# A hybrid decoder layer on one core: attention stages entered at a pair's first product, gate loads as a step, one x block made earlier, output operands on other x blocks

## Chip, cores and metric

One core of a Trainium2 chip runs the kernel. The metric is device time in microseconds (us); a time of the kernel is the median of its runs. TensorE (PE) has two granted clock levels in these records, 2.4 GHz (1.0) and 1.2 GHz (0.5). PE multiplies, VectorE (DVE) and ScalarE (ACT) prepare weights and take results away, SyncE (SP) issues nearly all DMAs. Each engine executes its own queue in the order in which the program puts the instructions there, and waits at the first one whose operands are not ready.

## What is computed

```python
xn = rmsnorm(h, g_pre)                       # h: 16 meta tokens + 512 tokens, 2048 wide
p = xn @ w_in                                # columns: q k v z_gla r hc gate_b gate_c z_conv
q, k, v, z_gla, r, hc, gate_b, gate_c, z_conv = split(p)
log_a = log_sigmoid(r @ w_gate_up + b_gate) / 16
o = gla_chunked(q * 128 ** -0.5, k, v, log_a)   # 4 heads, S_t = diag(exp(log_a)) S + k^T v
y_gla = rmsnorm(o, g_gla_out) * silu(z_gla)
y_conv = gate_b * causal_dwconv(gate_c * hc, w_conv) * silu(z_conv)
y = concat([y_gla, y_conv]) @ w_out
out = (h + rmsnorm(y, g_post))[16:]
```

All is float32. The kernel keeps that precision by splitting each operand into a rounded high half and the rest (low half) and summing three products: high by high, high by low, low by high.

## The kernel before

**Pairs and products.** The columns of `w_in` are cut into tiles of 128. After a start that multiplies six tiles plainly, two tiles at a time form a `Pair` (names such as `k1q1`, `z4z5`), and the pair is computed by a scheme of seven half-size products instead of eight, in the order `P5 P1 P6 P2 P3 P7 P4` (line 38). Each product needs one block of x, made once as high and low halves (`block`, line 502; arrays `xa`, `xb`, `xt`), and one block of weights per pair. A product is 24 matmuls of 256 to 264 columns: eight slices times three half-products. P2 accumulates onto the PSUM bank of P1 and P3 onto that of P5, so P2 can start only when ACT has copied P1's result away (`q`, line 256), and P3 only when it has copied P5's (`f`, line 253).

**Preparing weights.** `prepare` (line 202) adds or subtracts two raw tiles on DVE where the scheme wants it (P5, P6 and P3 at line 183, P7 at line 213), then `split` (line 114) makes the high half on ACT (`whi`, line 118) and the low half on DVE (`wlo`, line 119), into three buffers each. Next-pair loads are issued in the `prepare` of P5, P6 and P4 alone. The main loop (line 729) prepares two products ahead (`AHEAD = 2`), multiplies, and calls `away` (line 248), which takes results away.

**Attention stages.** Five generators per head are woven into the pairs: `decay` (letter d, line 583; nine steps, mostly DVE and three table functions on ACT), `gla_b` (t, transposes and scores), `gla_c` (s, states), `gla_d` (o, output and its norm) and `gla_e` (g, gate: loads `silu(z)` from DRAM, transposes, multiplies). A step ends at a `yield`. `away` runs `per` steps after each product and all that is left after P4. `before` stages enter at P5 and must be through at P2; `stages` enter at P2 (line 262). Which head's stages ride on which pair is the table at lines 358 to 367. Finished gates `silu(z)` go to DRAM (`zd`, line 301) and come back in `gla_e` (line 716); the two `z` buffers serve both.

**Order.** The program hands its instructions to a scheduler that puts them in order on each engine, with later code able to pass earlier code where it fits; the listings in the section on the change show the result.

**End.** After the last pair (`b7s7`) the mixed operand `ycat` is split into `ygh, ygl, ych, ycl` (lines 741 to 747), in the memory that the x blocks leave free, and PE computes the output projection in 16 blocks of 48 matmuls, 512 columns wide.

Of the kernel before, what the change touches and what calls it, by code (L numbers as in the profile page):

```python
# [9 lines left out]
F32 = mybir.dt.float32  # L10
# [5 lines left out]
P = 128  # L16
D = 2048
# [10 lines left out]
NP = S // P  # L28
# [3 lines left out]
XHALF = L // 2  # L32
NB = 8
# [9 lines left out]
def hymba_kernel(ctx, tc, xT, x, g_pre, w_r, w_t, w_up, b_gate, g_gla, w_conv, w_o, g_post, out):  # L43
# [10 lines left out]
    g1 = left.enter_context(tc.tile_pool(name="g1", bufs=1))  # L54

    def bank(name):
        return ps.tile([P, 512], F32, tag="bank", name=name)

    def mm(out_, lhsT, rhs, start, stop, **kw):
        nc.tensor.matmul(out_, lhsT, rhs, start=start, stop=stop, **kw)  # L60
# [36 lines left out]
    xa = [xp.tile([P, 2, NB, XHALF], F32R, tag=f"xa{i}", name=f"xa{i}") for i in range(2)]  # L97
# [70 lines left out]
    left_over = []  # L168
    STAGE = {}
# [3 lines left out]
    def step(n):  # L173
        for _ in range(n):
            while left_over:
                try:
                    next(left_over[0])
                    break
                except StopIteration:
                    left_over.pop(0)  # L180
# [4 lines left out]
    class Pair:  # L185
# [37 lines left out]
        def multiply(self, name, two):  # L223
            hi, lo = two
            (xh, xl), s = xc[name]
            c0, w = self.c0, self.w
            bank_of = {"P2": "P1", "P3": "P5"}.get(name)
            if bank_of:
                pt = self.sb[bank_of]
            else:  # L230
                pt = bank(f"{self.na}{self.nb}{name}")[:, 0:w]
                self.sb[name] = pt
            kw = {"skip_group_check": True} if bank_of else {}
            for k in range(NB):
                mm(pt, hi[:, k, :], xh[:, s, k, c0:], k == 0 and not bank_of, False, **kw)
                mm(pt, hi[:, k, :], xl[:, s, k, c0:], False, False, **kw)
                mm(pt, lo[:, k, :], xh[:, s, k, c0:], False, k == NB - 1, **kw)
# [10 lines left out]
        def away(self, name):  # L248
            sb = self.sb
            if name == "P5":  # L250

                left_over.extend(STAGE[g[0]](int(g[1])) for g in self.before)
                A.copy(self.tmp("f"), sb["P5"])
            elif name == "P1":

                A.copy(self.tmp("q"), sb["P1"])
            elif name == "P6":
                V.tensor_tensor(out=self.tmp("u"), in0=sb["P6"], in1=sb["q"], op=ALU.subtract)
            elif name == "P2":
                if self.before:  # L260
                    step(1000)
                left_over.extend(STAGE[g[0]](int(g[1])) for g in self.stages)
                self.dst_a, self.dst_b = self.dst()
                for o, s, e in self.dst_a[0]:
                    A.copy(o, sb["P1"][:, s - self.c0:e - self.c0])
            elif name == "P3":
                self.put(self.dst_a[1], sb["P5"], sb["u"], ALU.subtract)
            elif name == "P7":
                v = self.tmp("v")
                V.tensor_tensor(out=v, in0=sb["u"], in1=sb["P7"], op=ALU.subtract)  # L270
                self.put(self.dst_b[1], v, sb["f"], ALU.subtract)
            else:
                self.put(self.dst_b[0], sb["v"], sb["P4"], ALU.subtract)

    def prepare_next():
        n = len(ready)
        if n < len(line):
            p, i, name = line[n]
            at = line.index((p, 0, ORDER[0])) + len(ORDER)
            ready.append(p.prepare(name, line[at][0] if at < len(line) else None))  # L280
# [16 lines left out]
    def silu(*js):  # L297
        for j in js:
            z = zs.pop(j)
            A.activation(z, z, AF.Silu)  # L300
            nc.sync.dma_start(zd[:, j, :], z)
# [4 lines left out]
    def k_q(h, **kw):  # L306
        Pair(f"k{h}", f"q{h}", 0, lambda: (new_k(h), new_q(h)), **kw)

    def v_v(h, **kw):
        Pair(f"v{2 * h}", f"v{2 * h + 1}", 0, lambda: (new_v(2 * h), new_v(2 * h + 1)), **kw)  # L310

    def z_z(h, **kw):
        Pair(f"z{2 * h}", f"z{2 * h + 1}", NM // 2, lambda: (new_z(2 * h), new_z(2 * h + 1)),
             done=lambda: silu(2 * h, 2 * h + 1), **kw)
# [42 lines left out]
    def all_pairs():  # L357
        z_z(1)
        k_q(1, before=("d0",), per=3)
        v_v(1, before=("t0",), stages=("s0", "o0"))  # L360
        z_z(2, stages=("g0", "d1"), per=3)
        k_q(2, stages=("t1", "s1", "o1"), per=3)
        v_v(2, stages=("g1", "d2"), per=3)
        z_z(3, stages=("t2", "s2", "o2"), per=3)
        k_q(3, stages=("g2",))
        v_v(3, stages=("d3",))
        conv(0, ("t3", "s3"), ("o3", "g3"))
        for j in range(1, 8):
            conv(j)


    with tc.tile_pool(name="ini", bufs=1, reuse_waits="tile") as ini:
# [43 lines left out]
        for kt in range(KT):  # L416
# [7 lines left out]
            if kt == 10:  # L424
                for n in range(2):
                    t = slice(n * XHALF, (n + 1) * XHALF)
# [16 lines left out]
        def new_k(h):  # L443
            kn[h] = g1.tile([P, L], F32, tag="kn", name="kn")
            return natural(kn[h])

        def new_q(h):
            qn[h] = g1.tile([P, L], F32, tag="qn", name="qn")[:, 0:S]
            return main_only(qn[h])

        def new_v(j):
            t = g1.tile([P, L], F32, tag=f"vt{j % 2}", name="vt")
            vt.setdefault(j // 2, []).append(t)
            return natural(t)

        def new_z(j):
            zs[j] = gla.tile([P, S], F32, tag="z", name="z", bufs=2)
            return main_only(zs[j])
# [43 lines left out]
        def block(name, two, s, src):  # L502
            xc[name] = (two, s)
            for k in HK:
                A.copy(two[0][:, s, k, :], src[:, k])
                V.tensor_tensor(out=two[1][:, s, k, :], in0=src[:, k],
                                in1=two[0][:, s, k, :].bitcast(F32), op=ALU.subtract)
# [13 lines left out]
        tt = ini.tile([P, NB, XHALF], F32, name="tt")  # L521
# [12 lines left out]
        do_plain("z1", None)  # L534
        silu(0, 1)
        all_pairs()
        prepare_next()
        prepare_next()
        block("P1", xa, 0, b11)
        multiply(0)  # L540
        prepare_next()
        block("P2", xb, 0, b21)
# [1 line left out]
        prepare_next()  # L544
        multiply(2)
        block("P3", xb, 1, b22)
        prepare_next()
        block("P4", xa, 1, tt)
        first = 3


# [160 lines left out]
    def gla_e(h):  # L712
        on = st[h]
        zt = [gla.tile([P, S], F32, tag="z", name="z", bufs=2) for _ in range(2)]
        for e in range(2):
            nc.sync.dma_start(zt[e], zd[:, 2 * h + e, :])
        for e in range(2):
            ot = bank(f"ot{h}{e}")
            for p in range(NP):
                nc.tensor.transpose(ot[:, p * P:(p + 1) * P], on[:, p, e * P:(e + 1) * P], ident)  # L720
            z = zt[e]
            V.scalar_tensor_tensor(out=z, in0=ot, scalar=gg[:, e:e + 1], in1=z,
                                   op0=ALU.mult, op1=ALU.mult)
            nc.sync.dma_start(yd[:, 2 * h + e, :], z)
            yield


    STAGE.update(d=decay, t=gla_b, s=gla_c, o=gla_d, g=gla_e)
    for n in range(len(line)):
        while len(ready) < min(len(line), n + 1 + AHEAD):  # L730
            prepare_next()
        if n >= first:
            multiply(n)
        away(n)
# [3 lines left out]
    NC = 4  # L738
    NW = D // NC
    yp2 = ctx.enter_context(tc.tile_pool(name="yp2", bufs=1, side="right", reuse_waits="tile"))  # L740
    ygh, ygl, ych, ycl = (yp2.tile([P, 8, S], F32R, name=n) for n in ("ygh", "ygl", "ych", "ycl"))
    yg = yp2.tile([P, NP, D], F32, name="yg")
    for hi, lo, src in ((ygh, ygl, ycat["g"]), (ych, ycl, ycat["c"])):
        for k in range(0, 8, 2):
            A.copy(hi[:, k:k + 2], src[:, k:k + 2])  # L745
# [119 lines left out]
```

## Time and profile before

| | |
|---|---|
| median of 3 runs | 842.11 us (841.1 to 842.98) |
| profiled execution | 844.2 us, of it 842.5 us span |
| mean granted PE clock | 0.988 |
| busy: PE, DVE, ACT | 812.3, 621.1, 394.7 us |

The span is the time from the first to the last instruction. A view of waits says for how long an engine stood still and which instruction of which engine ended that. In a timeline each line is start, duration, engine, line of the code, operation, operands; what stands in brackets is idle time just before it and its releaser. A fast DVE operation may be recorded as longer than the distance to the next one's start; the distance is what it costs in a full queue.

### The profile page before, as it was taken

The page shows a single profiled execution, that of the slowest core. Times are in us where ns is not written, and L with a number is a line of the kernel's source. Part 1 is how long each engine was busy: PE and PEld are TensorE (multiplying, and loading weights), DVE is VectorE, ACT ScalarE, POOL GpSimd, SP SyncE. Part 2 cuts the span into 40 slices and gives each one's busy share as a digit, 9 for nine tenths or more (in the row PEclk, how much of TensorE's full clock was granted, in tenths as well). Part 3 has the DMA queues.
Part 4 walks back from the last instruction along what each step waited for, and adds up shares of the span by engine and source line. Part 5 has one row for each costly group of instructions (what it writes and reads, how often), then busy time and mean ns, then how long its engine had stood idle before and what let it go on. Part 6 is the DMA issues. An engine that isn't in the chain of part 4 may idle for free.

```text
span 842.5 us, 14191 instructions
## 1 busy us (share of the span) xinstructions
PE 812.3 (96%) x5980; PEld 769.4 (91%) x5980; DVE 621.1 (74%) x770; ACT 394.7 (47%) x547; POOL 2.3 (0%) x14
## 2 busy tenths in 40 slices
PE   8999898998989998999999999999998999999996
PEld 7999898997989998999999999999998788888886
DVE  6999989788799778979888878787877723140433
ACT  7635575485475465454444444444445622130311
POOL 0000000000000000000000000000000000000000
PEclk9999999998999999999999999999999999999999
DMA  8612222243133431263333333333334705050154
GB/s 288 210 52 86 96 96 98 76 151 114 62 117 127 156 104 50 76 224 102 101 101 119 105 115 115 118 106 100 102 100 145 274 19 187 1 200 0 51 182 168
DMA packets 30560, 98.92 MB, mean 117 GB/s; under 512 B 3904, under 2 KB 4800, under 8 KB 29728
## 3 DMA queue, kind: packets, MB, share of 16 engines
q1 hardware_dynamic: 28912, 94.86, 34.2%
q10 hardware_dynamic: 1584, 3.15, 1.0%
q8 instruction: 47, 0.77, 0.4%
q14 instruction: 17, 0.14, 0.1%
HBM read 89.61 MB, written 8.39 MB: 116 GB/s over the span
## 4 chain that ended last, share of the span: by engine, by line
PE 82%; DVE 8%; ACT 5%; issue 3%; DMA 2%; SPq 0%; DVEq 0%; ACTq 0%
PE out L60 21%; PE v L60 3%; PE k3q3P L60 2%; PE v2v3P L60 2%; PE h7c7P L60 2%; PE h5c5P L60 2%; PE h2c2P L60 2%; PE h6c6P L60 2%; PE h4c4P L60 2%; PE h3c3P L60 2%; PE h1c1P L60 2%; PE b3s3P L60 2%; PE b6s6P L60 2%; PE b5s5P L60 2%; PE b4s4P L60 2%
## 5 line engine op out<-in xcount | busy, mean ns | idle before, releaser
L118 ACT CAST whi<-raw 128x1024 fp32r<-128x1024 f32 x207 | 216.4, 1051 | 222.7 <-DVE raw L183 94.2
L119 DVE TENSOR_TENSOR wlo<-raw,whi 128x1024 fp32r<-128x1024 f32 x207 | 251.9, 1222 | 49.1 <-ACT whi L118 45.3
L183 DVE TENSOR_TENSOR raw<-raw 128x1024 f32<-128x1024 f32 x75 | 90.1, 1221 | 4.6 <-DMA raw<-in_w_t_dram 3.8
L791 DVE TENSOR_TENSOR yg<-out,gpost 128x512 f32<-128x512 f32 (+1 forms) x17 | 11.2, 659 | 110.3 <-ACT junk L790 110.2
L790 ACT ACTIVATE junk<-out 128x512 f32<-128x512 f32 (+1 forms) x17 | 9.7, 572 | 120.7 <-PE out L60 120.7
L60 PE MATMUL out<-whi,ygh 128*128 128x512 f32 (+1 forms) x136 | 52.0, 386 | 2.5 <-ACT ygh L745 2.5
L60 PE MATMUL out<-whi,ygl 128*128 128x512 f32 (+1 forms) x136 | 52.7, 388 | 0.3 <-DVE ygl L746 0.3
L60 PE MATMUL out<-wlo,ygh 128*128 128x512 f32 (+1 forms) x136 | 52.5, 386 | 0.0
L60 PE MATMUL out<-wlo,ych 128*128 128x512 f32 (+1 forms) x136 | 51.9, 381 | 0.0
L60 PE MATMUL out<-whi,ych 128*128 128x512 f32 (+1 forms) x136 | 51.9, 381 | 0.0
L60 PE MATMUL out<-whi,ycl 128*128 128x512 f32 (+1 forms) x136 | 51.9, 381 | 0.0
L60 PEld LDWEIGHTS out<-whi,ygh 128*128 128x128 f32 x136 | 25.9, 191 | 8.3 <-ACT ygh L745 2.7
L60 PEld LDWEIGHTS out<-whi,ygl 128*128 128x128 f32 x136 | 25.9, 190 | 6.4 <-DVE ygl L746 0.8
L60 PEld LDWEIGHTS out<-wlo,ygh 128*128 128x128 f32 x136 | 25.9, 191 | 5.6
L213 DVE TENSOR_TENSOR raw<-raw 128x1024 f32<-128x1024 f32 x25 | 30.6, 1223 | 0.6
L60 PEld LDWEIGHTS out<-wlo,ych 128*128 128x128 f32 x136 | 25.5, 188 | 5.5
L60 PEld LDWEIGHTS out<-whi,ycl 128*128 128x128 f32 x136 | 25.5, 188 | 5.5
L60 PEld LDWEIGHTS out<-whi,ych 128*128 128x128 f32 x136 | 25.5, 187 | 5.5
L129 ACT CAST whi<-raw 128x1024 fp32r<-128x1024 f32 (+2 forms) x13 | 11.0, 850 | 20.2 <-PE v L60 12.5
L60 PE MATMUL k2q2P<-xt,whi 128*128 128x264 f32 x48 | 10.3, 315 | 4.0 <-ACT whi L118 4.0
L130 DVE TENSOR_TENSOR wlo<-raw,whi 128x1024 fp32r<-128x1024 f32 (+2 forms) x13 | 12.5, 970 | 0.8 <-ACT whi L129 0.8
L60 PE MATMUL h0c0P<-xt,whi 128*128 128x258 f32 x48 | 10.4, 316 | 2.8 <-ACT whi L118 2.8
(663 smaller groups left out, 2319.4 us busy)
## 6 DMA issues: line engine op xcount, KB each, us to landing
raw<-in_w_t_dram SPq DMA_DIRECT2D x108, 512.0 KB, 4.1
raw<-in_w_o_dram SPq DMA_DIRECT2D x32, 512.0 KB, 4.8
xres<-in_x_dram SPq DMA_DIRECT2D x4, 1024.0 KB, 6.4
xr<-in_xT_dram SPq DMA_DIRECT2D x7, 528.0 KB, 6.5
z<-zd SPq DMA_DIRECT2D x8, 256.0 KB, 3.7
yd<-z SPq DMA_DIRECT2D x8, 256.0 KB, 3.7
yg<-yd SPq DMA_DIRECT2D x1, 2048.0 KB, 8.1
out_dram<-yg SPq DMA_DIRECT2D x8, 256.0 KB, 2.5
```

Source lines behind the costliest of these rows:

```text
L60: nc.tensor.matmul(out_, lhsT, rhs, start=start, stop=stop, **kw)
L118: A.copy(hi, raw)
L119: V.tensor_tensor(out=lo, in0=raw, in1=hi.bitcast(F32), op=ALU.subtract)
L129: A.copy(hi[:, k, :], raw[:, k, :])
L130: V.tensor_tensor(out=lo[:, k, :], in0=raw[:, k, :], in1=hi[:, k, :].bitcast(F32), op=ALU.subtract)
L183: V.tensor_tensor(out=a, in0=a, in1=b, op=ALU.add)
L213: V.tensor_tensor(out=raw["11"], in0=raw["11"], in1=raw["22"], op=ALU.subtract)
L790: nc.scalar.activation(junk, pt, AF.Square, accum_out=s_)
L791: nc.vector.tensor_tensor(out=yg[:, t, cs], in0=pt, in1=gpost[:, cs], op=ALU.mult)
```

## The change

Four edits. (1) A pair's `stages` now enter at P5 if the pair has no `before` stages, and the pairs that had `per=3` without `before` fall back to two steps per product. (2) `gla_e` yields once after issuing its two loads, so that loads and transposes are different steps. (3) In the start of the paired part, `block("P4", ...)` moves from the end to a place right after `block("P1", ...)`, and one `prepare_next()` (that of the first pair's P3) is dropped there, so that the main loop prepares it. (4) In the memory of the x blocks, `yg` now comes first, over the two `xa` arrays, and `ygh, ygl, ych, ycl` after it, on `xb` and `xt`.

```diff
             if name == "P5":
-                left_over.extend(STAGE[g[0]](int(g[1])) for g in self.before)
+                left_over.extend(STAGE[g[0]](int(g[1])) for g in self.before or self.stages)
                 A.copy(self.tmp("f"), sb["P5"])
...
                 if self.before:
                     step(1000)
-                left_over.extend(STAGE[g[0]](int(g[1])) for g in self.stages)
+                    left_over.extend(STAGE[g[0]](int(g[1])) for g in self.stages)
...
-        z_z(2, stages=("g0", "d1"), per=3)
-        k_q(2, stages=("t1", "s1", "o1"), per=3)
-        v_v(2, stages=("g1", "d2"), per=3)
-        z_z(3, stages=("t2", "s2", "o2"), per=3)
+        z_z(2, stages=("g0", "d1"))
+        k_q(2, stages=("t1", "s1", "o1"))
+        v_v(2, stages=("g1", "d2"))
+        z_z(3, stages=("t2", "s2", "o2"))
...
         block("P1", xa, 0, b11)
+        block("P4", xa, 1, tt)
         multiply(0)
...
         block("P3", xb, 1, b22)
-        prepare_next()
-        block("P4", xa, 1, tt)
         first = 3
...
             nc.sync.dma_start(zt[e], zd[:, 2 * h + e, :])
+        yield
...
+    yg = yp2.tile([P, 4 * NB * XHALF], F32, name="yg")[:, 0:NP * D].rearrange(
+        "p (t d) -> p t d", d=D)
     ygh, ygl, ych, ycl = (yp2.tile([P, 8, S], F32R, name=n) for n in ("ygh", "ygl", "ych", "ycl"))
-    yg = yp2.tile([P, NP, D], F32, name="yg")
```

How the order on the engines moves, at the three places that the prediction speaks of. First ACT at the first pair, `z2z3`; `whi<-raw` is the high half of a weight block, `f` and `q` are the copies that P3 and P2 wait for:

```order
 L300 ACTIVATE raw<-raw 128x512
-L118 CAST whi<-raw 128x1024 x3
-L253 COPY f<-z2z3P_1028 128x256
-L256 COPY q<-z2z3P_1064 128x256
-L118 CAST whi<-raw 128x1024
-L265 COPY z<-z2z3P_1064 128x256
+L118 CAST whi<-raw 128x1024 x2
+L253 COPY f<-z2z3P_1032 128x256
+L256 COPY q<-z2z3P_1068 128x256
+L118 CAST whi<-raw 128x1024 x2
+L265 COPY z<-z2z3P_1068 128x256
```

The two copies now stand before the third high half (P3's), no longer behind it.

DVE at the same place before, from the last x blocks of P3 (`xb`) on; `xa<-tt` is half of P4's block, `u` takes P6 away, L213 is P7's subtraction:

```order
L506 TENSOR_TENSOR xb_100<-xr,xb_99 128x1056 x2
L183 TENSOR_TENSOR raw<-raw 128x1024
L506 TENSOR_TENSOR xa_98<-tt,xa_97 128x1056
L119 TENSOR_TENSOR wlo<-raw,whi 128x1024
L258 TENSOR_TENSOR u<-z2z3P_1093,q 128x256
```

Here P4's half block stands ahead of P3's low half (the L119). The same stretch after, from the same x blocks to P3's low half:

```order
L506 TENSOR_TENSOR xb_100<-xr,xb_99 128x1056 x2
L183 TENSOR_TENSOR raw<-raw 128x1024
L258 TENSOR_TENSOR u<-z2z3P_1097,q 128x256
L213 TENSOR_TENSOR raw<-raw 128x1024
L119 TENSOR_TENSOR wlo<-raw,whi 128x1024
```

P4's half block has left this stretch (it stands earlier), and P3's low half now comes behind `u` and P7's subtraction.

DVE around the pair `z4z5`, which carries gate g0 and decay d1, before; the rows run from the result of P7 (`v`) into the next pair's weights:

```order
L270 TENSOR_TENSOR v<-u,z4z5P_2087 128x256
L604 TENSOR_TENSOR eqk<-B 128x512
L607 TENSOR_TENSOR esx<-B 128x512
L610 TENSOR_TENSOR esx<-B 128x16
L612 TENSOR_TENSOR esx<-B 128x4x64
L613 TENSOR_TENSOR esx<-B 128x4x64
L119 TENSOR_TENSOR wlo<-raw,whi 128x1024
L722 SCALAR_TENSOR_TENSOR z<-ot_2019,gg,z 128x512
L246 TENSOR_TENSOR z<-v,f 128x256
```

The decay's exponents (L604 on) and the gate's second half (L722) stand behind P7's result here. After, in the middle of the same pair, from P6's result (`u`) to P7's low half:

```order
L258 TENSOR_TENSOR u<-z4z5P_1978,q 128x256
L596 TENSOR_TENSOR esx<-B,esx 128x528
L213 TENSOR_TENSOR raw<-raw 128x1024
L119 TENSOR_TENSOR wlo<-raw,whi 128x1024
L597 SCALAR_TENSOR_TENSOR B<-keep,esx 128x528
L119 TENSOR_TENSOR wlo<-raw,whi 128x1024
```

The decay's operation on the logarithm (now L596) has moved ahead of P7's subtraction (L213) and P3's low half (the first L119), its scan (L597) between that and P7's low half, and its exponents follow there; both gate operations stand further up.

## Rows read from the trace of the kernel before

**Rows 1.** Waits of PE: waiting line, releaser: total us, times, longest.

```profile
PE k2q2P L60 <- ACT whi L118: 4.0, 1, 4.0
PE h0c0P L60 <- ACT whi L118: 2.8, 1, 2.8
PE z2z3P L60 <- ACT f L253: 2.6, 1, 2.6
PE out L60 <- ACT ygh L745: 2.5, 1, 2.5
...
PE z6z7P L60 <- ACT whi L118: 1.6, 1, 1.6
PE z6z7P L60 <- DVE wlo L119: 1.5, 1, 1.5
```

**Rows 2.** Four stretches: length, busy (x count) by engine, PEclk, DMA share, GB/s.

```profile
96.00:103.00 7.00, 4.41 (x26) 4.20 (x25) 6.92 (x8) 2.64 (x4) 0.53 (x1) 0.76 0.23 82
...
191.00:202.00 11.00, 7.00 (x40) 6.57 (x39) 9.44 (x13) 6.70 (x10) 0.00 (x0) 0.69 0.42 134
245.00:254.00 9.00, 5.93 (x48) 5.41 (x48) 8.49 (x13) 5.61 (x11) 0.00 (x0) 1.00 0.16 60
319.00:332.00 13.00, 9.58 (x65) 9.06 (x65) 11.81 (x17) 6.51 (x12) 0.00 (x0) 0.87 0.14 40
```

**Rows 3.** Timeline of ACT at the first pair.

```profile
97.50 1.04 ACT L118 CAST whi<-raw 128x1024 fp32r<-128x1024 f32 x1 [5.02 <-DVE raw L183]
...
98.72 0.38 ACT L256 COPY q<-z2z3P 128x256 f32<-128x256 f32 x1
```

**Rows 4.** Timeline of DVE at the first pair.

```profile
97.31 1.25 DVE L506 TENSOR_TENSOR xa<-tt,xa 128x1056 fp32r<-128x1056 f32 x1
98.58 1.23 DVE L119 TENSOR_TENSOR wlo<-raw,whi 128x1024 fp32r<-128x1024 f32 x1
99.72 0.42 DVE L258 TENSOR_TENSOR u<-z2z3P,q 128x256 f32<-128x256 f32 x1
100.06 1.22 DVE L213 TENSOR_TENSOR raw<-raw 128x1024 f32<-128x1024 f32 x1
```

**Rows 5.** Pieces of the chain that ended last: start us, us, what.

```profile
411.21 20.03 PE h2c2P L60 x168
```

**Rows 6.** The same chain at 286 us, the transposes of one gate.

```profile
286.13 0.87 PE ot L720 x8
```

**Rows 7.** Timeline of ACT in `z4z5`: the decay's first functions.

```profile
177.64 0.86 ACT L591 ACTIVATE esx<-zp,bg 128x264 f32<-128x264 f32 x2
178.52 1.28 ACT L595 ACT_TABLE_LOAD   x1
179.81 0.65 ACT L595 ACTIVATE esx<-esx 128x528 f32<-128x528 f32 x1
```

**Rows 8.** Timeline of DVE at the end of decay d1.

```profile
192.92 0.69 DVE L633 TENSOR_TENSOR B<-B,qn 128x512 f32<-128x512 f32 x1
193.52 1.22 DVE L183 TENSOR_TENSOR raw<-raw 128x1024 f32<-128x1024 f32 x1
...
195.85 2.36 DVE L119 TENSOR_TENSOR wlo<-raw,whi 128x1024 fp32r<-128x1024 f32 x2 [0.51 <-ACT whi L118]
```

**Rows 9.** The chain that ended last at 185 us: a gate's load.

```profile
185.75 3.25 DMA z<-zd
```

**Rows 10.** DMA issues by line: engine, operation, count, KB each, us to landing.

```profile
z<-zd SPq DMA_DIRECT2D x8, 256.0 KB, 3.7
...
zd<-z SPq DMA_DIRECT2D x6, 256.0 KB, 2.8
```

**Rows 11.** The tile `z`, all its DMAs.

```profile
DMA to landing us min/median/max: 2.0/3.1/5.6
```

**Rows 12.** Timeline of ACT after the last pair.

```profile
651.64 0.62 ACT L344 ACTIVATE sg<-sg 128x512 f32<-128x512 f32 x1
652.17 1.98 ACT L745 CAST ygh<-yg 128x1024 fp32r<-128x1024 f32 x2
```

## Prediction

> **What bounds the kernel now.** I read the table of busy times first: PE works 812.3 of 842.5 us, so a change can only win what PE loses. The view of PE's waits [rows 1] tells where: nearly all of its long waits end with a weight half made by ACT or DVE, and they lie where a pair that carries a decay ends and the next begins (`k2q2`, `z6z7`, `h0c0`), at the first pair (`z2z3`) and before the output projection (`out`). The windows around four of these places [rows 2] give what each costs. Idle time is length less PE's busy time: 2.6 us at the first pair, 4.0 at `k2q2`, 3.1 at `z6z7`, 3.4 at `h0c0`. DVE is busy for most of each window (6.92 of 7.00 at the first pair). The PEclk column shows a second loss: a mean of 0.76 over 7 us is 7 x 0.24 / 0.5 = 3.4 us at the lower level (1.2 GHz), 0.69 over 11 us is 6.8 us, 0.87 over 13 us is 3.4 us; at `z6z7` it stays 1.00. Work at the lower level takes twice its time, so of the part in which PE works half is lost: 1.5 of about 3 us after the restart at the first pair, 2.5 of about 5 at `k2q2` (restart near 196, when the whi of [rows 8] is there), 1.7 at `h0c0`. Together the places cost 4.1 (A, first pair), 6.5 (C, `k2q2`), 3.1 (D, `z6z7`) and 5.1 us (E, `h0c0`).
>
> For scale: an undisturbed pair of seven products takes 20.03 us [rows 5], so a product 2.86 and a matmul 0.12.
>
> **Edit 3, the first pair (A).** Before, P6's end is followed by 2.6 us of waiting for ACT's copy `f` [rows 1], since ACT, in its queue, sat idle for 5.0 us in front of P3's high half at 97.50 and made the copies only behind it, at 98.45 and 98.72 [rows 3]. Now the copies stand ahead of that cast, both sources are long done, and P2 starts when P6 ends, at 96.3. The wait does not vanish: P3 is next. P3's low half ran from 98.58 [rows 4]; in the new order P4's half block (97.31 to 98.58) has moved ahead, at equal cost in a queue that is full anyway, while `u` and P7's subtraction (99.72 to 101.2 together, 0.34 + 1.14) come ahead of it. So it ends at about 99.8 + 1.5 = 101.3. PE has P2 until 99.15 and three matmuls (0.36) that need high halves alone: it waits 101.3 - 99.15 - 0.36 = 1.8 us, in pieces, as the third of these also needs P7's high half. Gain 4.1 - 1.8 = **2.3 us**, if the clock holds through pieces of that size. The dropped `prepare_next` issues no load (only P5, P6 and P4 do), so no queue is passed by a DMA.
>
> **Edits 1 and 2 at `z4z5`, which sets C.** Removed: nothing; the nine decay steps and the gate cost DVE and ACT the same, and no table load goes or comes. What moves is the start, from P2 to P5, four products or so less crowding at the end. Before, the next pair's P6 addition stood behind the whole decay, from 193.52 on, and its low half came after 195.85 [rows 8]. Before, DVE also waited for a gate's operand, whose load began at 185.75 and took 3.25 us [rows 9] because it was asked for only then; with edit 2 and the earlier start the loads stand in SP's queue right behind the stores that free their buffers, two pairs ahead, so g0 finds its operand there.
>
> Two points must now be met. *First, P3's low half.* PE passes the gate's first transposes after P5, the second and the decay's two small matmuls after P1. From there ACT needs 0.9 for the absolute values, 1.3 for a table load, 0.55 for the exponential [rows 7], and as much again for the logarithm: 4.6 us. Then DVE, where L596 is ahead in the queue: 0.6 for a 512-wide operation (spacing from 192.92 to 193.52 in [rows 8]), 1.14 for P7's subtraction, 1.14 for P3's low half (spacing 98.58 to 99.72 [rows 4]): 7.5 us. Behind that L596 are queued P7's and P3's weights, and PE waits for those. PE has P6, P2 and three matmuls meanwhile, 5.7 + 0.4 = 6.1: it waits **1.4 us**. *Second, the next pair's P6.* From P3's low half on DVE has five low halves and one addition (6 x 1.14), the rest of the decay (a scan of some 1.2, seven 512-wide at 0.6, four 256-wide at 0.34 and a tiny one: 6.9), four evictions at 0.34 and one transposed operand of 0.5: 15.6 us. PE has the rest of P3 (2.6), P7, P4 and two products of the next pair (11.4) and fourteen transposes (1.5, at 0.87 for eight [rows 6]): 15.5 us. Level: I allow **0.5 us** for waits between the engines. C then costs 1.9 instead of 6.5: gain **4.6 us**.
>
> **`v4v5` (D) and `v6v7` (E).** `v4v5` carries g1 and d2 in the same order, `v6v7` d3 without a gate and with the decay a product earlier. By likeness both keep 1.9 us: gains 3.1 - 1.9 = **1.2** and 5.1 - 1.9 = **3.2 us**. The bounds of that 1.9: 0 where DVE gets ahead, 4.6 if the whole function chain is exposed. `k1q1` and `v2v3` (1.8 and less on waits) keep their rows and their cost.
>
> **Gate g2 in `k3q3`, a new wait.** It now starts at P5, directly behind the pair that makes z6 and z7. z7 is finished at about 2.6 us after that pair's P4 (eviction, table load 1.28, function 0.65), then its store takes 2.8 and the load 3.7 [rows 10]: 9.1. DVE waits for it at the second gate operation, and behind that stand P7's subtraction and P3's low half: with 0.7 + 2 x 1.14 that is 12.1 to 12.6. PE needs that half after four products, one gate's transposes and two matmuls: 11.4 + 0.9 + 0.2 = 12.5. I take **0.5 us** lost; if both transfers land as late as the slowest, 5.6 [rows 11], it is 4 us more. SP's raw loads behind these transfers need buffers that come free later still; without that cover each would wait 2.8.
>
> **Edit 4, the output operands: zero.** ACT begins the first split at 652.17, directly behind the gate's silu at 651.64 [rows 12]. What holds it is its place in ACT's queue, not the memory, and its place is the same in the new order. The 2.5 us of `out` [rows 1] stay.
>
> **Sum.** 2.3 + 4.6 + 1.2 + 3.2 - 0.5 = 10.8 us off the span of 842.5, about 831.7; the 1.7 us between span and profiled execution do not change. The median of runs, 842.1, is close to the span: **831.3 us**. The forecast's own range is 828 to 835.
>
> **A rule against it.** The load of a table takes 1.28 us and the function follows 0.01 us later, at 179.81 [rows 7]. The Trainium skill (ScalarE: Activation LUTs, section What ACT_TABLE_LOAD costs) counts some 1.38 us of drain on top, about 2.66 us a switch. By it the function chain would be 2.8 us longer, and as an estimate from that page the three pairs would lose 8 us more. This trace shows no such drain behind the load, so the sum goes by the rows.
>
> **Rivals.**
> *The clock falls in the new waits.* The level fell where PE stood 2.6 to 4 us, and stayed at `z6z7` with two waits of 1.5 and 1.6 [rows 1, 2]. The new waits (1.4 to 1.8, a second one later) are of that kept kind, but close. Each fall costs 1.5 to 2.5 us; with two or three: 831.3 + 5 = 836.3 us. Chance 0.22.
> *The function chain starts late, slower than before.* Abs stands in ACT's queue behind weight casts. If these wait for a raw tile or a buffer, the whole chain, then DVE's L596, and with it P7's and P3's weights shift, in all three pairs. With 3 us each the waits exceed 4 us, the clock falls too (2.5): 831.3 + 3 x 5.5 = 847.8 us. It decides from about 2 us of delay plus the fall in each (3 x 3.6 makes up for the gain). Against it: before, ACT idles between its casts there, and its row for Abs at 177.64 follows work without a gap [rows 7]. Chance 0.05.
> *Edit 4 does what its place suggests,* and the split starts at P3's end: up to 2.5 + 1.7 us (idle, and clock as at E) more: 827.1. The silu row speaks against it. Chance 0.03.
> *The new waits do not appear,* as DVE is ahead by more than I count: 3 x 1.9 less: 825.6. Chance 0.07.
> The forecast keeps 0.63.
>
> **How the numbers follow.** The range runs from the edge between the last two cases, 826, to 838, which holds most of the clock case and a late g2 by itself; outside are the slower case and the rims, below 0.2 together. A difference under 0.2%, 1.7 us, cannot be told from none. Faster 0.92 (all but the slower case and a rim of the clock case), same 0.03, slower 0.05.
>
> **What would show it.** In the waits of PE after, the entries of 4.0 and 2.8 for `k2q2` and `h0c0` and `f` at `z2z3` are gone; entries of 1 to 2 us appear at P3 of `z2z3`, `z4z5`, `v4v5` and `v6v7` with a low or high half as releaser; `out` keeps its 2.5. Window clocks at A, C and E read 1.00. DVE shows no wait for `z<-zd` in `z4z5`, perhaps one in `k3q3`. I am wrong if clocks near 0.8 remain in windows of that length, if the waits at P3 exceed 3 us, or if gains appear at the output.

## The result, and the profile after

The changed kernel took 834.95 us (median of 4 runs, 832.84 to 835.1), the kernel before 842.0 beside it: a ratio of 0.991 (95% interval 0.9891 to 0.993). Measured again beside other kernels it took 835.86 (833.45 to 837.95, before 841.45, ratio 0.9931, 0.9909 to 0.9953). So the change wins 5.6 to 7.1 us. The forecast was 831.3 in a range of 826 to 838.

The profiled execution spans 833.1 us, against 842.5 before. The waits of PE, in the same view as [rows 1] (waiting line, releaser: total us, times, longest):

```profile
PE out L60 <- ACT ygh L747: 2.5, 1, 2.5
PE k1q1P L60 <- DVE wlo L119: 2.1, 1, 2.1
PE z2z3P L60 <- ACT q L256: 2.0, 1, 2.0
PE z4z5P L60 <- ACT whi L118: 1.6, 1, 1.6
PE v4v5P L60 <- ACT whi L118: 1.6, 1, 1.6
PE v6v7P L60 <- DVE wlo L119: 1.2, 1, 1.2
...
PE b0s0P L60 <- ACT whi L118: 1.0, 1, 1.0
```

The 4.0 us of `k2q2`, the 2.8 of `h0c0` and the two of `z6z7` are gone. In their place stand 1.6 at `z4z5`, 1.6 at `v4v5` and 1.2 at `v6v7`; `out` has kept its 2.5; `z2z3` waits 2.0 for another copy; `k1q1` and `b0s0` wait longer than before. At `k1q1` and `v2v3`, whose products are woven into each other, the waits have changed their form. Before:

```profile
PE k1q1P L60 <- DVE wlo L119: 1.8, 2, 1.2
PE v2v3P L60 <- ACT whi L118: 1.6, 1, 1.6
```

After, beside the single 2.1 us above:

```profile
PE v2v3P L60 <- ACT whi L118: 0.5, 1, 0.5
```

So PE waits less there in all (2.6 us instead of 3.4), but 2.1 us of it in one piece.

The windows of after that answer to [rows 2] (length, busy by PE, PEld, DVE, ACT, POOL, then PEclk, DMA share, GB/s), at `z2z3`, `k1q1`, `z4z5`, `v4v5` and `out`:

```profile
94.00:101.00 7.00, 5.04 (x42) 4.84 (x42) 7.00 (x8) 3.74 (x6) 0.53 (x1) 1.00 0.11 29
120.00:128.00 8.00, 5.84 (x34) 5.42 (x32) 7.90 (x15) 6.91 (x11) 0.00 (x0) 0.79 0.23 67
174.00:182.00 8.00, 6.42 (x40) 6.02 (x39) 7.51 (x11) 5.78 (x8) 0.00 (x0) 0.79 0.36 99
227.00:233.00 6.00, 4.44 (x35) 4.14 (x35) 5.41 (x6) 4.96 (x6) 0.00 (x0) 1.00 0.18 50
...
640.00:650.00 10.00, 7.19 (x30) 5.55 (x29) 8.81 (x10) 8.59 (x10) 0.00 (x0) 0.83 0.88 327
```

A PEclk of 0.79 over 8 us is 8 x 0.21 / 0.5 = 3.4 us at 1.2 GHz. It stands at `k1q1` and at `z4z5`; the first pair now keeps 2.4 GHz. At `k1q1` the clock held before:

```profile
125.00:133.00 8.00, 5.70 (x43) 5.16 (x44) 7.89 (x16) 6.84 (x14) 0.00 (x0) 1.00 0.23 67
```

To compare places I use one number more, the **loss**: the distance from one matmul's start to the next, less the distance at 2.4 GHz (0.12 us for 256 columns), summed over a pair. It holds waits and half clock together. In the four rows from `k1q1` to `h0c0` it also holds, in both kernels, about 2 to 3 us each in which the small matmuls of the attention stages start further apart than their columns alone take. The last two columns are two executions of the changed kernel.

| loss by place, us | before | after | after, again | gain forecast | gain measured, twice |
|---|---|---|---|---|---|
| up to the first pair | 7.3 | 6.0 | 5.4 | 0 | 1.3, 2.0 |
| `z2z3` (A) | 4.1 | 2.2 | 3.7 | 2.3 | 2.0, 0.4 |
| `k1q1` and `v2v3` | 6.1 | 7.3 | 6.2 | 0 | -1.2, 0.0 |
| `z4z5` and `k2q2` (C) | 8.7 | 5.9 | 4.7 | 4.6 | 2.8, 4.0 |
| `v4v5` to `k3q3` (D, gate g2) | 6.7 | 4.9 | 4.9 | 1.2 - 0.5 | 1.8, 1.7 |
| `v6v7` and `h0c0` (E) | 7.4 | 4.0 | 4.0 | 3.2 | 3.4, 3.4 |
| `b0s0` | 1.0 | 1.9 | 1.9 | 0 | -0.9, -0.9 |
| `b7s7` and `out` | 5.3 | 5.2 | 5.2 | 0 | 0.1, 0.1 |
| sum | 46.1 | 36.7 | 35.3 | 10.8 | 9.4, 10.8 |

The thirteen pairs from `h1c1` to `h7c7` are left out; they hold -0.6 us in all, the same in each column.

The first row is not the change's: up to the first pair the engines' orders are the same in both kernels but for DVE's last operation, and the 1.3 and 2.0 us there are the chance of single executions. Three things need an explanation: the places where two executions of one kernel differ, the new loss at `k1q1`, which is the clock's and not that of more waiting, and why the sum of the traces is larger than the gain of the medians.

### The profile page after: what moved, and what is told of

Read it like the earlier page. It is cut to its first block, busy times and chain, and to the rows that moved or that the text cites. A ratio compares the mean times of both kernels' runs of the same rounds, so it can differ in the third digit from the quotient of the medians.

```text
span 833.1 us, 14189 instructions
## 1 busy us (share of the span) xinstructions
PE 810.2 (97%) x5980; PEld 767.8 (92%) x5980; DVE 619.8 (74%) x770; ACT 394.9 (47%) x547; POOL 2.3 (0%) x14
## 4 chain that ended last, share of the span: by engine, by line
PE 85%; DVE 7%; ACT 4%; DMA 2%; issue 2%; SPq 0%; DVEq 0%; ACTq 0%
PE out L60 22%; PE v L60 3%; PE k2q2P L60 2%; PE k3q3P L60 2%; PE v2v3P L60 2%; PE h0c0P L60 2%; PE b0s0P L60 2%; PE h7c7P L60 2%; PE h6c6P L60 2%; PE h4c4P L60 2%; PE h1c1P L60 2%; PE h5c5P L60 2%; PE h3c3P L60 2%; PE h2c2P L60 2%; PE b2s2P L60 2%; PE b6s6P L60 2%
## 5 line engine op out<-in xcount | busy, mean ns | idle before, releaser
L119 DVE TENSOR_TENSOR wlo<-raw,whi 128x1024 fp32r<-128x1024 f32 x207 | 251.9, 1221 | 43.9 <-ACT whi L118 41.1
L213 DVE TENSOR_TENSOR raw<-raw 128x1024 f32<-128x1024 f32 x25 | 30.5, 1221 | 0.5
L334 DVE SCALAR_TENSOR_TENSOR y<-hh,wc,y 128x512 f32<-128x512 f32 x16 | 12.0, 749 | 0.3
L812 DVE SCALAR_TENSOR_TENSOR yg<-yg,rs,xres 128x512 f32<-128x512 f32 (+1 forms) x17 | 11.1, 716 | 0.1
```

Of the source, the lines that this page charges most:

```text
L119: V.tensor_tensor(out=lo, in0=raw, in1=hi.bitcast(F32), op=ALU.subtract)
L213: V.tensor_tensor(out=raw["11"], in0=raw["11"], in1=raw["22"], op=ALU.subtract)
L334: V.scalar_tensor_tensor(out=y, in0=hh[:, i:i + S], scalar=wc[:, j, i:i + 1], in1=y, op0=ALU.mult, op1=ALU.add)
L812: nc.vector.scalar_tensor_tensor(out=yg[:, t, qs], in0=yg[:, t, qs], scalar=rs, in1=xt[:, qs], op0=ALU.mult, op1=ALU.add)
```

## Experiments

### Edit 3 alone

```diff
         block("P1", xa, 0, b11)
+        block("P4", xa, 1, tt)
...
         block("P3", xb, 1, b22)
-        prepare_next()
-        block("P4", xa, 1, tt)
```

> The kernel before with edit 3 alone (block P4 of x beside P1, one preparation fewer in the start). In the changed kernel PE's loss at z2z3 fell from 4.1 to 2.2 us, but from 3.2 to 4.8 us it rose at k1q1, where DVE waits 2.97 us (before 1.61) for a raw weight block. Theory 1, the transfer: that block is late because edit 1 put a gate's load ahead of it in SP's queue. Without edit 1 the block comes 2 us sooner with everything else: DVE waits 1.6 us for it, k1q1 keeps a loss near 3.2, and edit 3 is worth its full 2.0 us: 840.0 us. Theory 2, a full DVE: what PE gains at z2z3 it waits for at k1q1 whatever SP does: DVE's wait for the block about 3, loss at k1q1 4.5 to 5, edit 3 worth 0.3 to 0.8 us: 841.2 to 841.7.

840.16 us against 841.86 (ratio 0.9977, 0.9959 to 0.9994). The loss at `z2z3` is 2.2 and that of `k1q1` 3.2, as before; DVE waits 1.48 us for the block. Edit 3 wins its 2.0 us at the first pair and keeps it: theory 1 by the trace; of the medians, 1.7 us apart, the interval reaches from 0.5 to 3.5.

### Edit 1 alone

```diff
-                left_over.extend(STAGE[g[0]](int(g[1])) for g in self.before)
+                left_over.extend(STAGE[g[0]](int(g[1])) for g in self.before or self.stages)
...
-        z_z(2, stages=("g0", "d1"), per=3)
+        z_z(2, stages=("g0", "d1"))
...
```

> The kernel before with edit 1 alone (stages enter at P5, two steps per product). The queue of SP then has the gate's loads in the same places as the changed kernel. Theory 1 (transfer): the wait of DVE for the raw block in k1q1 is near 3.0 us although z2z3 is as before, and PE loses 1.4 us or more beyond the 3.2 of before at k1q1. Theory 2 (full DVE): k1q1 as before, loss 3.2. In both the waits of 4.0 at k2q2 and 2.8 at h0c0 are gone, waits of 1.4 to 1.8 stand at P3 of z4z5, v4v5 and v6v7: 842.1 - 2.9 - 1.4 - 3.2 + 0.9 (b0s0) = 835.5 us with theory 2, 836.9 and more with theory 1.

838.17 us against 841.86 (ratio 0.9961, 0.9946 to 0.9977). DVE's wait for the block is 3.32 us although z2z3 is as before, and `k1q1` and `v2v3` lose 9.2 us together instead of 6.1. That is theory 1 again, though part of these 9.2 us is a fall of the clock at `v2v3`. The time is 1.3 us more than the least that this theory gave: without edit 2 `z4z5` loses 5.0, and in this execution the clock fell at `v2v3`, `z4z5` and `v6v7`.

The chain shows in the queue of SP. In the changed kernel (start, duration, engine, line, operation):

```profile
104.51 0.33 SPq L301 DMA_DIRECT2D zd<-z  x1
109.29 0.33 SPq L715 DMA_DIRECT2D z<-zd  x1
109.67 0.42 SPq L199 DMA_DIRECT2D raw<-in_w_t_dram  x1
```

and of DVE there, from its timeline, with the idle time before in brackets:

```profile
114.53 1.23 DVE L183 TENSOR_TENSOR raw<-raw 128x1024 f32<-128x1024 f32 x1 [2.97 <-DMA raw<-in_w_t_dram]
```

With edit 3 alone:

```profile
105.23 0.33 SPq L301 DMA_DIRECT2D zd<-z  x1
109.89 0.33 SPq L199 DMA_DIRECT2D raw<-in_w_t_dram  x1
...
113.77 1.23 DVE L183 TENSOR_TENSOR raw<-raw 128x1024 f32<-128x1024 f32 x1 [1.48 <-DMA raw<-in_w_t_dram]
```

Edit 1 brings the load of gate g0 (L715) so far forward that it stands in SP's queue before the weight block of `k1q1`. In the changed kernel it waits for the store of z to land (4.8 us after its issue at 104.51), and then its 256 KB move while the block's 512 KB do. The block can be used 4.86 us after its issue instead of 3.88, and is issued 5.16 us after that store instead of 4.66.

### The gates' loads on another queue

```diff
-            nc.sync.dma_start(zt[e], zd[:, 2 * h + e, :])
+            nc.gpsimd.dma_start(zt[e], zd[:, 2 * h + e, :])
```

> The changed kernel with the gates' loads issued by GpSimd instead of SP. In the changed kernel SP holds the next raw load of k1q1 for 0.5 us behind the gate's load, and the block then takes 4.9 us to land instead of 4.0. If the place in SP's queue is what costs, DVE's wait for the block in k1q1 falls from 2.97 to about 2.5 us and further to 1.6 if the gate's transfer no longer lies beside it; PE's loss at k1q1 falls from 4.8 towards 3.2 and the time to 833.4 to 834.5. If only the shared transfer capacity costs, the wait stays near 2.5 to 3.0 and the time at 835.

836.46 us against 841.86 (ratio 0.9931, 0.9908 to 0.9955), the same as the changed kernel within the spread. The block is issued 4.66 us after the store again, and DVE's wait falls to 2.32, but it still takes 4.7 us to be there. So of the 1.5 us that DVE waits longer about 0.6 was the place in the queue. The rest stays while the gate's transfer lies beside the block's; that this is the reason is likely and not shown by one execution. In this execution `v6v7` waited 2.1 us instead of 1.2 for a late raw block.

### The gate's load behind the block

```diff
+            if h == 0:
+                A.copy(zt[e][:, 0:1], kn[1][:, 0:1])
             nc.sync.dma_start(zt[e], zd[:, 2 * h + e, :])
```

> The changed kernel, where the loads of gate g0 must wait for the first keys of k1q1 (a copy of one column on ACT writes into their buffers first), so that they stand behind the weight loads of v2v3 in SP's queue and no longer ahead of the block that k1q1 waits for. Nothing else moves. Theory 1 (the transfer costs): DVE's wait for the block 1.5 instead of 2.97 us, PE's wait at k1q1 1.4 instead of 2.3, the losses of k1q1 and v2v3 together 6.1 instead of 7.3: 833.7 us. Theory 2 (DVE's work is the limit there): sum of the two still 7 or more, 834.5 to 835.5.

832.92 us against 841.45 (ratio 0.99, 0.9881 to 0.9919). DVE waits 1.51 us, `k1q1` and `v2v3` lose 6.2 together:

```profile
112.62 1.23 DVE L183 TENSOR_TENSOR raw<-raw 128x1024 f32<-128x1024 f32 x1 [1.51 <-DMA raw<-in_w_t_dram]
```

Theory 1 for the place. In this profile the clock fell at `out` alone. For the median it is less certain: 2.0 to 2.9 us under the changed kernel, whose own runs spread over 5 us.

### The changed kernel once more

> The changed kernel once more, beside the next two on one chip. The same waits as in its first profile: 2.1 at z2z3, 2.3 at k1q1, 1.7 at z4z5 and v4v5, 1.4 at v6v7, 1.2 at b0s0, 2.6 at out, each within 0.1 us, since its queues are the same. Theory 1 (which waits are followed by a fall of the clock is not fixed by their length): the set of stretches at the lower level differs from the first profile's in at least one place, and the time by 1.3 to 3 us with it. Theory 2 (the clock follows the waits' lengths): the same stretches at the lower level, k1q1, z4z5 and out, time 834.9 within 0.6.

835.86 us, with a span of 831.7 in its profile. At `z2z3`, `z4z5`, `v4v5`, `v6v7`, `b0s0` and `out` the waits are the same within 0.1 us, as both theories had it. But `k1q1` did not repeat:

```profile
105.44 0.33 SPq L301 DMA_DIRECT2D zd<-z  x1
108.36 0.33 SPq L715 DMA_DIRECT2D z<-zd  x1
110.10 0.33 SPq L199 DMA_DIRECT2D raw<-in_w_t_dram  x1
...
114.04 1.23 DVE L183 TENSOR_TENSOR raw<-raw 128x1024 f32<-128x1024 f32 x1 [1.54 <-DMA raw<-in_w_t_dram]
```

Here the store landed after 2.9 us instead of 4.8, the gate's load went out 1.7 us before the block's, and the block was there in 3.94. So the loss at `k1q1` is not there in every execution. Over all profiles: with the gate's load on SP's queue ahead of the block, DVE had it 4.8 to 5.7 us after its issue in six executions, in which the store took 3.3 to 4.9 us, and 3.94 in this one; without, 3.9 to 4.3 in five. That the store's landing decides it rests on this one execution and is not shown.

The clock did not repeat either. The windows of this execution at `z2z3`, `k1q1` and `z4z5`:

```profile
94.00:101.00 7.00, 5.04 (x30) 4.83 (x29) 7.00 (x8) 3.15 (x6) 0.53 (x1) 0.77 0.11 36
120.00:128.00 8.00, 5.09 (x40) 4.66 (x39) 7.88 (x15) 7.46 (x11) 0.00 (x0) 1.00 0.22 67
174.00:182.00 8.00, 6.41 (x52) 6.00 (x51) 7.73 (x11) 6.77 (x10) 0.00 (x0) 1.00 0.36 114
```

PE is busy for the same 5.04 of 7.00 us at `z2z3` and 6.4 of 8.00 at `z4z5` as in the first execution, with PEclk 0.77 where it was 1.00 and 1.00 where it was 0.79. Theory 1: a wait of one length is followed by a fall in one execution and not in another.

### The memory of the copy f

```diff
     g1 = left.enter_context(tc.tile_pool(name="g1", bufs=1))
+    ev0 = left.enter_context(tc.tile_pool(name="ev0", bufs=1, reuse_waits="tile"))
...
-            self.sb[name] = ev.tile(
+            self.sb[name] = (ev0 if name in "fq" else ev).tile(
```

> The changed kernel with the buffers of f and q in memory of their own, opened early, instead of memory that the raw x leaves. In the changed kernel f of the first pair starts at 96.19, when DVE has read the raw x for the last time, and P2 stands 2.0 us for q behind it. Theory 1 (DVE's queue sets z2z3): the wait for q goes, P2 starts when P6 ends at 94.7, and PE then waits about 2 us at P3 for its low half, which stands in DVE's queue until 99.8: the pair's loss stays at 2.0 to 2.3, time 835.0. Theory 2 (the memory sets it): the loss at z2z3 falls to 0.5 or less, time 833.3 or less.

835.81 us against 841.86 (ratio 0.993, 0.9908 to 0.9952). In the changed kernel's timeline of ACT both copies stand at the head of the queue, and yet:

```profile
96.19 0.37 ACT L253 COPY f<-z2z3P 128x256 f32<-128x256 f32 x1 [5.06 <-DVE xb L506]
96.46 0.38 ACT L256 COPY q<-z2z3P 128x256 f32<-128x256 f32 x1
```

`f` has nothing to do with `xb`, but it lies where the raw x lay, and the last operation on `xb` is the last reader of that. With memory of its own (this kernel's timeline of ACT; its lines are one higher):

```profile
92.25 0.37 ACT L257 COPY q<-z2z3P 128x256 f32<-128x256 f32 x1 [0.57 <-PE z2z3P L61]
97.34 1.05 ACT L119 CAST whi<-raw 128x1024 fp32r<-128x1024 f32 x1 [4.71 <-DVE raw L184]
```

q is ready at 92.6 and PE's wait for it is down to 0.2 us. The loss of the pair is 2.0 all the same: about 1.5 us of it now stands where P3 and P7 begin, and P3's high half, at 97.34, had waited 4.71 us for its operand from DVE. Theory 1: DVE's queue sets this pair, and the wait only changes its place.

### Without edit 2

```diff
             nc.sync.dma_start(zt[e], zd[:, 2 * h + e, :])
-        yield
```

> The changed kernel without edit 2 (the gate's loads and its first transposes are one step again). The queue of SP is the same in both, so the loads stand in the same places. Theory 1 (edit 1 alone brings the loads forward, edit 2 moves only the transposes): no wait of DVE for a gate's operand at z4z5, losses at z4z5 and v4v5 within 0.5 us of the changed kernel's 3.9 and 2.1, time 834.5 to 835.8. Theory 2, that of the prediction (edit 2 is what has the operand there in time): DVE waits up to 3.2 us for the operand at z4z5 and PE loses 1.5 us or more beyond the changed kernel: 836.5 or more.

838.39 us against 841.68 (ratio 0.9965, 0.995 to 0.998). Neither theory. No wait of DVE for a gate's operand, so theory 2 is out, but the time is 2.6 us above what theory 1 allowed. Of that the waits explain little. DVE's timeline at `z4z5` shows one part:

```profile
176.90 1.22 DVE L213 TENSOR_TENSOR raw<-raw 128x1024 f32<-128x1024 f32 x1
178.04 1.25 DVE L597 TENSOR_TENSOR_SCAN B<-keep,esx 128x528 f32<-128x528 f32 x1
179.21 1.20 DVE L119 TENSOR_TENSOR wlo<-raw,whi 128x1024 fp32r<-128x1024 f32 x1
```

With both transposes in one step the order shifts, and the decay's scan stands ahead of P3's low half: PE waits 0.5 us more there. `z6z7` and `k3q3` wait 0.2 and 0.5 more, `v4v5` 1.1 less: 0.1 us in all. `h1c1` waits 0.5 us, but it does so too in the kernel with other memory for f, which has edit 2. Most of the profile's difference is clock: a fall at `z2z3` behind the unchanged wait, and one at `z4z5` that lasted twice as long (6.8 us). Why the median of ten runs is that much higher I leave open.

### The decay ahead of the gate

```diff
-        z_z(2, stages=("g0", "d1"))
+        z_z(2, stages=("d1", "g0"))
...
-        v_v(2, stages=("g1", "d2"))
+        v_v(2, stages=("d2", "g1"))
```

> The changed kernel with the decay ahead of the gate in z4z5 and v4v5 (stages d1, g0 and d2, g1). The chain of functions then starts behind P5 and not behind the gate's transposes and P1, some 3 us earlier, and the loads of gate g0 leave k1q1. Theory 1 (the residual wait is the chain's length; k1q1 loses to the gate's transfer): waits at P3 of z4z5 and v4v5 fall from 1.7 to under 0.5, DVE's wait for the raw block in k1q1 from 2.97 to 1.5, the loss at k1q1 from 4.8 to 3.2: 835 - 1.6 - 2 x 1.2 and up to 1.7 for the clock at z4z5: 829.3 to 831. Theory 2 (the work of DVE is the same and comes out later): the gate's operations, late now, stand ahead of the next pair's weights: new waits of 1.5 us or more at the end of z4z5 and v4v5 or at the start of the next pair: 833 to 836.

838.06 us against 841.68 (ratio 0.9959, 0.9943 to 0.9975): 2 to 3 us slower than the changed kernel. The half of theory 1 on `k1q1` held (DVE's wait 1.80, loss 3.2). The other half fell. The waits of PE:

```profile
PE v4v5P L60 <- ACT whi L118: 2.8, 1, 2.8
...
PE z4z5P L60 <- ACT whi L118: 1.8, 1, 1.8
...
PE z4z5P L60 <- DVE wlo L119: 1.3, 1, 1.3
```

This execution reaches the pair 0.7 us later than the changed kernel's. The functions come earlier all the same (DVE's L596 at 173.45 instead of 174.49), but then the scan and the decay's five differences stand ahead of P7's subtraction on DVE, which starts at 178.65 instead of 175.11. So the length of the function chain is not what the residual wait can be cut by; the work of DVE comes out at the same pair, as theory 2 said, though not at its end but at P3 and P7. The time is 2 us above the range of that theory; around the 2.8 us at `v4v5` the clock was at 1.2 GHz for 6.8 us.

### The split of the gated output earlier

```diff
+        if n == len(line) - 1:
+            xp_cm.__exit__(None, None, None)
+            yp2 = ctx.enter_context(tc.tile_pool(name="yp2", bufs=1, side="right",
+                                                 reuse_waits="tile"))
...
+            split_y(ygh, ygl, ycat["g"])
         away(n)
...
-            got.append(split(raw, [P, 2, NW], wp if seq[0] % 9 < 3 else wq))
+            got.append(split(raw, [P, 2, NW], wp if (seq[0] + 1) % 9 < 3 else wq))
```

> The changed kernel with the split of the gated attention output (ygh, ygl) put into the program ahead of the last pair's end, and with the first two instead of three output weight blocks in the pair's weight buffers, so that on ACT the split stands behind the second of these casts and not behind the third and the silu. Theory 1 (the 2.6 us at out are set by the place in ACT's queue): ygh starts while PE multiplies the last P4, the wait for ygh goes; what is late next is ygl, which stands on DVE behind P4's result, 0.4 + 1.2 us: a wait near 1.6 instead of 2.6 and 0.5, and no fall of the clock behind it if that wait is short enough: 833.4 (clock falls) to 831.8. Theory 2 (something else holds out): 835 or more, as the third weight block is then late.

832.13 us against 841.68 (ratio 0.9895, 0.9871 to 0.992), faster than the changed kernel. ACT in the changed kernel, at the end of the last pair:

```profile
641.41 1.04 ACT L118 CAST whi<-raw 128x1024 fp32r<-128x1024 f32 x1 [1.79 <-PE b7s7P L60]
642.36 0.62 ACT L344 ACTIVATE sg<-sg 128x512 f32<-128x512 f32 x1
642.89 1.98 ACT L747 CAST ygh<-yg 128x1024 fp32r<-128x1024 f32 x2
```

The third output weight block waits for the buffer that P4 leaves, and with it all behind it. With the split ahead of it:

```profile
638.17 1.05 ACT L118 CAST whi<-raw 128x1024 fp32r<-128x1024 f32 x1 [1.79 <-PE b7s7P L60]
639.12 3.88 ACT L734 CAST ygh<-yg 128x1024 fp32r<-128x1024 f32 x4
...
PE out L60 <- DVE ygl L735: 0.7, 1, 0.7
```

What is left is 0.7 us for ygl, and PEclk is 1.00 there. `b7s7` and `out` lose 1.5 us instead of 5.2. Theory 1, with less left over than the 1.6 expected.

> The same without edit 4: ygh lies over the x blocks of P1 and P4 again and must wait for P4's last product. Theory 1: now the memory decides, ygh starts when P4 ends and not before, its first part and that of ygl take 1.0 + 1.2 us: a wait near 2.2 at out, 0.6 us more than with edit 4: 834.0 or, where the clock holds, 832.4. Theory 2, that of the prediction taken further (edit 4 is worth nothing in any order): the same time and the same wait as with edit 4.

The edit takes the old order of the four operands and yg. 832.96 us against 841.68 (ratio 0.9904, 0.9876 to 0.9932). The cast of ygh now waits for PE:

```profile
645.41 3.90 ACT L734 CAST ygh<-yg 128x1024 fp32r<-128x1024 f32 x4 [1.91 <-PE b7s7P L60]
...
PE out L60 <- ACT ygh L734: 1.1, 1, 1.1
```

The two places lose 2.1 us, 0.6 more than with edit 4: theory 1 by the trace, though the wait of 1.1 us is half of the 2.2 that it gave (the medians, 0.8 apart, do not separate the two). So edit 4 is worth nothing in the order of the change, where ACT's queue is in front, and 0.6 us once it is not.

### Both remedies

> Early split of the gated output and the later loads of gate g0 together. The two places are 480 us apart and should add: the wait at out 0.9 instead of 2.6 and 0.5 and, without a fall of the clock there, 3.7 us; at k1q1 and v2v3 1.2 us: 834.95 - 4.9 = 830.0 us, 829 to 832.5 with one fall of the clock less or more. Rival (the clock takes back what a wait gives): 832 or more, as the early split alone.

831.14 us against 841.45, ratio 0.9876 (0.9856 to 0.9896): the fastest kernel of this study, 3.8 to 4.7 us under the changed one. 1.1 us of the expected gain is missing; in its profile the clock fell at `z2z3` and at `v6v7`, where PE waited 2.1 us for a low half behind a late raw block, and at `out` and `k1q1` it held. It is within the range that I gave, and by its medians not told apart from the two single remedies.

## Why the prediction was right, point by point

**What bounds the kernel.** Right. From the first pair on the gain came out of PE's waits and the clock behind them; the pairs from `h1c1` on are the same to 0.1 us.

**Edit 3, the first pair.** The size is right where the clock held: 2.0 us in four profiles, against 2.3. In the six others it fell behind the new wait, and 0.4 us was left. Of waiting itself the edit removes 0.6 us, 2.6 to 2.0; the rest of the 2.0 is the fall that stood behind the wait of before, and with edit 1 alone the clock held behind that same 2.6 us (loss 2.9). So some of this gain is luck. The way was wrong too. The prediction said that the copies' sources "are long done, and P2 starts when P6 ends". P2 started 2.0 us later, since `f` waited for memory that I had not looked at. Once that is taken away most of the wait is where I had put it, at P3 and P7, so the sum held: DVE's queue would have given the same.

**Edits 1 and 2 at `z4z5`.** The first wait was put at 1.4 us and is 1.6 by the row. Its chain is as worked out; ACT's functions, Abs at 169.68 to the end of the logarithm, take 4.8 us instead of 4.6, and DVE's L596, P7's subtraction and P3's low half follow in that order. The second wait, 0.5 us at the next P6, did not come. What failed is the clock: the prediction let it hold through waits "of that kept kind". In the first profile it fell behind the 1.6 us, and the gain of C was 2.8; in the second it held, and the gain was 4.0. One of the prediction's own signs of being wrong came up here, clocks near 0.8: 0.79 at C in the first profile, 0.77 at A in the second.

**`v4v5`, `v6v7`, gate g2.** By likeness 1.9 us each; 1.6 and 1.2 by the rows. The 0.5 us for gate g2 did not appear, so D came out better than forecast.

**Queues moved past.** This step failed. The prediction looked at gate g0's load where it is used ("g0 finds its operand there", which is so) and at SP's loads behind the transfers only at `k3q3`. But the load had moved ahead of the block of `k1q1`. In the six profiles in which the block came late for it, `k1q1` and `v2v3` lost 0.6 to 3.1 us more than before, 1.2 in the changed kernel. PE's waits there did not grow in the changed kernel; they fell together into one of 2.1 us, and the clock fell behind it.

**`b0s0`** was counted as unchanged and costs 0.9 us more. With the stages entering at P5, the norm of o3 comes three products sooner, behind P5 instead of P2, and its table load stands on ACT ahead of the weight's cast that PE waits for:

```profile
343.40 1.28 ACT L703 ACT_TABLE_LOAD   x1
344.70 0.30 ACT L703 ACTIVATE ss<-ss,epst 128x4 f32<-128x4 f32 x1
345.28 1.04 ACT L118 CAST whi<-raw 128x1024 fp32r<-128x1024 f32 x1 [0.28 <-PE b0s0P L60]
```

The table load is not what held this cast: the norm was through at 345.00, and the cast stood another 0.28 us until PE released its buffer. So the norm's own time did not delay this cast. Which shift in the order makes the 0.9 us stays open.

Here too the function follows its table load at once (343.40 + 1.28 = 344.68, start 344.70): the drain that the Trainium skill (ScalarE: Activation LUTs, section What ACT_TABLE_LOAD costs) adds does not show behind it, and the three pairs did not lose the 8 us that the prediction had estimated from that page.

**Edit 4: zero.** Right, for the reason given: the wait of 2.5 us at `out` is the same with edit 4 and without it, and the early split took most of it away.

**The sum.** 10.8 us forecast; 9.4 and 10.8 by the two traces; 5.6 to 7.1 by the medians. Of the traces' gains 1.3 and 2.0 us lie ahead of the first pair, so 8.1 and 8.8 are left for the change, and that the second trace meets the 10.8 is luck. The step that was off in the sum is the last one, which took a trace's sum off the median. The traced execution of before, 844.2 us, is 2.1 above that median. It reaches the first pair at 87.59 us, the latest of thirteen profiles (85.62 to 87.59) although the order up to there is the same in all but for DVE's last operation, and the clock fell at four places in it, for 3.4 to 6.8 us each. What one execution loses by chance cannot be won by a change.

**The clock rival** (836.3, chance 0.22) came true in part, so that 834.95 lies nearer to it than to the forecast. Of the ten profiles that have the 2.0 us of `z2z3`, the clock fell behind it in six, at a price of 1.5 us (losses of 2.2 and 3.7). Behind the 1.6 us of `z4z5` it fell in four of eight, behind the equal wait of `v4v5` in none of eight, behind the 1.0 of `b0s0` in none. At `k1q1` it fell behind single waits of 1.8 to 2.1 us in six of seven profiles, and behind those of 1.2 to 1.4 in none of six. The chance was too low: by these counts it should have been spread as an expected 1.5 to 3 us, my estimate, over all new waits, and not kept as a case apart. That the time still lies inside the range is owed to the range's upper end, which had been set to hold most of this case.

## What to carry to other kernels

When a step starts earlier, follow its loads up the queue to where the program now puts them, and look at what stands behind them there: a load that comes in time for its own use can make another one late, in a place far from the edit. A wait that an edit removes can stay as a smaller one at the next thing that the same full engine delivers; moving the copy, its memory or the functions ahead of it did not shorten it here. And a sum made from one trace carries that execution's chance: set it against the median with two or three profiles of the same kernel, if there are any.

## What the runs showed of the hardware

Equal waits of PE were followed by a fall of its clock in one execution and not in another: 5.04 us busy of the same 7.00 at `z2z3`, granted 1.00 in one and 0.77 in the other, a difference of 1.5 us. A longer single wait was followed by a fall more often: at `k1q1` in six of seven profiles behind 1.8 to 2.1 us, in none of six behind 1.2 to 1.4. What decides it is left open here.

A 256 KB store landed after 4.8 us in one execution and 2.9 in the next, from the same place in the queue. The 512 KB block of `k1q1` was usable 3.9 to 4.3 us after its issue without the gate's 256 KB load ahead of it, and 4.8 to 5.7 in six of seven executions with it. Part of such a spread is the load's own: a raw load of the same 512 KB in `v6v7` landed after 3.6 to 5.4 us in eleven executions in which no other transfer was under way when it was issued. So how much of the difference between the two groups is the gate's transfer is not shown.
